# The low parts of split weights move from GpSimd to VectorE in each layer's first block

## The chip, the cores and the metric

The kernel runs on one core of one Trainium2 chip. The metric is device time in microseconds (us) of one execution of the whole program. Engines carry the names of the profile: PE (TensorE matmul), PEld (its weight loads), DVE (VectorE), ACT (ScalarE), POOL (GpSimd), SP (SyncE, which here only issues DMAs).

## What is computed

Two layers over one sequence of 2048 frames of width 1024. Each layer modulates and normalises its input, projects it once with a wide weight, runs two branches (gated linear attention and differential softmax attention) and projects their outputs back.

```python
for l in range(DEPTH):                       # DEPTH = 2
    mod = silu(c) @ w_ada[l] + b_ada[l]
    shift, scale, gate = jnp.split(mod, 3, axis=-1)
    h = rms_norm(x, norm_g[l]) * (1.0 + scale[:, None]) + shift[:, None]
    proj = h @ w_in[l]
    gq, gk, gv, glr, gz, dq, dk, dv, dz = split_columns(proj)
    gqkv = silu(causal_depthwise_conv(concat(gq, gk, gv), conv_w[l]))   # 4 taps
    o_gla = gla_branch(gqkv, glr, gz, ...)
    o_diff = diff_branch(dq, dk, dv, dz, ...)
    y = concat(o_gla, o_diff) @ w_out[l]
    x = x + gate[:, None] * y
```

## The kernel before

**Tiling.** The sequence is cut into four blocks of 512 frames (`u` = 0 to 3), so the program passes eight blocks, four for each layer (`l`). A block's dense work is nine items of eight weight tiles (`k`), each tile 128 x 512: four attention heads, two convolution groups and one gate from `w_in`, and two halves of `w_out`.

**Split weights.** Matmuls run on float32r, so each operand is kept as a high part (a rounded copy, float32r) and a low part (what is left of the float32 value), and three matmuls take the place of one: high by high, high by low, low by high. For a weight tile `weights()` does that (lines 586 to 599). In a layer's first block (`u` = 0) the raw tile comes in by DMA (`raw`, three buffers, 256 KB), ACT makes the high part into the first half of `w`, POOL subtracts it from `raw` to make the low part in the second half (line 596), and SP writes both halves to DRAM (`wd`, 512 KB). In the three later blocks the ready pair is read back (`w<-wd`) and no engine computes on it. `w` has four buffers. So the subtraction is done 2 layers x 9 items x 8 tiles = 144 times.

**Other work on these engines.** DVE does the convolution taps and their activation (`conv_evac`, tiles `ub`, `t`, `uT`, `qT`), the scores' maximum and copy out of PSUM (`s<-sc`), the mixing of the two softmax maps (`s<-s,r`), the low parts of the activations (`hlo`, `ql`, `ol`) and small statistics (`oss`, `qss`, `r`). POOL does small powers (`rq`, `wq`, `gw`, `xrs`), 64 x 64 memsets of `s`, and two kinds of 128 x 512 operation on tiles, `vN` and `rt`. `am` sums the columns of `w_ada` on DVE. `oh` and `ol` are the high and low part of the output projection's other operand, two buffers each.

**Order.** Operations are first recorded; `Program.order()` (line 199) then simulates the engines with a table of costs (`Program.cost`, line 171) and gives each engine the order in which it would take them, lowest recorded number first among those ready. Every engine then runs its list strictly in that order and waits at the first entry that isn't ready. For a 128 x 512 subtraction the planner reckons 100 + 2.2 x 512 = 1226 ns on POOL and 1.042 x 512 + 68 = 601 ns on DVE. SP's list is one queue as well: a `wd` write waits there for the low part, and the `raw` and `w<-wd` reads recorded after it wait behind it. All recorded operations carry line 305 (`issue`) in the profile, so they are told apart by their tiles.

Of the kernel before, what the change touches and what calls it, by code (L numbers as in the profile page):

```python
# [11 lines left out]
F32 = mybir.dt.float32  # L12
# [3 lines left out]
ALU = mybir.AluOpType  # L16
# [292 lines left out]
def trunk_kernel(ctx, tc, x, c, w_ada, b_ada, norm_g, w_in, conv_w, w_gk, b_gk, gla_norm_g,  # L309
# [28 lines left out]
    V, A, G, T, SY = (prog.queue(e) for e in "VAGTS")  # L338
# [247 lines left out]
    def weights(l, u, item, k, src, n=None):  # L586
        w = p_w.tile([P, 2, 512], F32R, tag="w", name="w")
        hi, lo = w[:, 0, :], w[:, 1, :]
        kept = WD[l][item][k]
        if u > 0:  # L590
            SY.dma_start(w.bitcast(F32), kept)
            return hi, lo
        raw = p_raw.tile([P, 512], F32, tag="raw", name="raw")
        SY.dma_start(raw if n is None else raw.rearrange("p (g n) -> p g n", n=n), src)
        A.copy(hi, raw)
        G.tensor_tensor(lo, raw, hi.bitcast(F32), op=ALU.subtract)
        if NU > 1:
            SY.dma_start(kept, w.bitcast(F32))
        return hi, lo
# [69 lines left out]
    def proj_T(l, u, item, col, banks):  # L669
        hhi, hlo = state["hhi"], state["hlo"]  # L670
        for k in range(KT):
            hi, lo = weights(l, u, item, k, w_in[l, k * P:(k + 1) * P, col:col + 512])
            for j in range(4):
                cs = slice(j * P, (j + 1) * P)
                if k == 0:
                    banks.append(acc())
                T.matmul(banks[j], hi[:, cs], hhi[k], start=(k == 0), stop=False)
                T.matmul(banks[j], hi[:, cs], hlo[k], start=False, stop=False)
                T.matmul(banks[j], lo[:, cs], hhi[k], start=False, stop=(k == KT - 1))
                yield pe(0.65)  # L680
# [387 lines left out]
    def dense_gen(l, u, items):  # L1068
# [12 lines left out]
        def head_proj(hd):  # L1081
            def ld(k):
                src = w_in[l, k * P:(k + 1) * P, C_D:C_D + 2048].rearrange("p (g n) -> p g n", n=512)
                return weights(l, u, hd, k, src[:, :, hd * P:hd * P + P], n=P)

            banks = []
            yield from proj_N(ld, banks)
            if hd == LAST:
                done("free_h", key + 1)
            if hd >= 1:  # L1090
                yield need("qkT", key, hd - 1)
            if hd >= 2:
                yield need("attn", key, hd - 2)
            head_evac(l, u, hd, banks)
            done("hev", key, hd)

        def gate_proj():
            banks = []
            yield from proj_N(lambda k: weights(l, u, 6, k, w_in[l, k * P:(k + 1) * P, C_GZ:C_GZ + 512]), banks)
            if LAST == 4:  # L1100
                done("free_h", key + 1)
            yield need("scan", key)
            osb = GL["osb"]
            for t in range(TT):
                sz = t2()
                silu2(sz, banks[t])
                G.tensor_tensor(osb[:, t, :], osb[:, t, :], sz, op=ALU.mult)
            done("gz", key)
# [135 lines left out]
```

## Time and profile before

| what | value |
|---|---|
| median of 3 runs | 2620.98 us (2617.81 to 2625.61) |
| the profiled execution's own time | 2622.21 us |
| its span in the profile | 2620.5 us |
| granted TensorE clock, mean | 0.992 |
| high parts `w` on ACT | 144, median 620 ns |
| low parts `w` on POOL | 144, median 1294 ns, longest 2534 ns |
| first and last low part start | 23.7 and 1620.3 us |

The profile is of one execution. A row of busy times counts an engine as busy from an instruction's start to its end, whether it computes or is held up in the middle. The rows of a group give its count, its total and the mean of one; the rows of waits give how long an engine stood idle and what ended it; the chain of waits follows the end of the program back to what released each step. The two stretches in which low parts are made are called the first and the second stage here: 20 to 340 us and 1310 to 1640 us.

### The profile page before, as it was taken

Reading aid. Unit: us, or ns where it says so; the run is one execution under the profiler, and the core shown is the slowest. Engines: PE = TensorE matmul, PEld = TensorE weight load, DVE = VectorE, ACT = ScalarE, POOL = GpSimd, SP = SyncE. Lnnn points to the kernel's source line nnn. Section 1 sums busy time; section 2 is a strip of 40 time slices with the busy share of each in tenths; the row PEclk is TensorE's granted clock in tenths of the full one; section 3 lists DMA queues with packets and bytes.
Section 4 is the critical chain, followed back from the end, with each engine's and each line's share of the span. In section 5 each row is a group of like instructions: output and inputs, shape, how many; then the busy total and the mean of one; then the engine's idle time right before and its main releaser. Section 6 shows DMA issues by size and latency. Waiting matters only on the chain.

```text
span 2620.5 us, 40701 instructions
## 1 busy us (share of the span) xinstructions
PE 2495.5 (95%) x13923; PEld 2031.5 (78%) x13923; DVE 1771.3 (68%) x5021; ACT 1215.3 (46%) x2592; POOL 608.3 (23%) x804
## 2 busy tenths in 40 slices
PE   6899899999999999999899999999999999999997
PEld 4676678877888778888677777888788887888786
DVE  4778847874667846677847874657737787377854
ACT  3555623554345543545634564344624556244442
POOL 2445421122010210102144554111111112110111
PEclk9999999999999999999999999999999999999998
DMA  8677586446553455344267767454374443743342
GB/s 283 225 235 256 200 302 198 161 166 211 178 181 125 158 171 189 133 140 149 81 237 248 245 214 253 169 179 156 126 268 155 143 157 113 254 141 129 101 149 89
DMA packets 201615, 476.11 MB, mean 182 GB/s; under 512 B 20736, under 2 KB 78272, under 8 KB 201408
## 3 DMA queue, kind: packets, MB, share of 16 engines
q1 hardware_dynamic: 201408, 473.51, 53.6%
q8 instruction: 111, 1.82, 0.3%
q14 instruction: 96, 0.79, 0.1%
HBM read 362.29 MB, written 111.15 MB: 181 GB/s over the span
## 4 chain that ended last, share of the span: by engine, by line
PE 71%; DVE 17%; DMA 3%; ACT 3%; issue 3%; POOL 1%; SPq 1%; DVEq 0%; ACTq 0%; POOLq 0%
PE acc L305 46%; PE sc L305 10%; PE po L305 8%; PE tp L305 7%; DVE s L305 6%; DVE t L305 3%; DMA wr<-in_w_ada_dram 1%; ACT s L305 1%; SPq L305 1%; DVE ql L305 1%; DVE am L305 1%; DVE hhi L305 1%; DMA w<-wd 1%; DVE r L305 1%; DVE hlo L305 1%
## 5 line engine op out<-in xcount | busy, mean ns | idle before, releaser
L305 PE MATMUL acc<-w,hhi 128*128 128x512 f32 x2560 | 835.0, 402 | 8.7 <-DMA w<-wd 4.3
L305 PEld LDWEIGHTS acc<-w,hhi 128*128 128x128 f32 x2560 | 464.8, 189 | 101.1 <-ACT ub L305 6.8
L305 PE MATMUL acc<-w,hlo 128*128 128x512 f32 x1280 | 504.9, 395 | 0.0
L305 ACT ACTIVATE s<-s,mx 128x512 f32<-128x512 f32 (+15 forms) x256 | 308.1, 1204 | 375.1 <-DVE s L305 372.3
L305 PE MATMUL acc<-hhi,w 128*128 128x512 f32 x1024 | 370.3, 402 | 0.6 <-DVE z L305 0.3
L305 PE MATMUL acc<-w,oh 128*128 128x512 f32 x1024 | 331.9, 401 | 12.1 <-DVE t L305 6.0
L305 DVE TENSOR_SCALAR_CACHE_REDUCE s<-sc,mx 64x64 f32<-64x64 f32 (+5 forms) x640 | 307.1, 485 | 37.8 <-PE sc L305 19.3
L305 POOL MEMSET s<- 64x64 f32 x256 | 38.9, 156 | 1111.1 <-DVE s L305 575.6
L305 PEld LDWEIGHTS acc<-w,hlo 128*128 128x128 f32 x1280 | 241.5, 189 | 48.9
L305 POOL TENSOR_TENSOR w<-raw,w 128x512 fp32r<-128x512 f32 x144 | 195.0, 1363 | 197.1 <-ACT w L305 180.7
L305 PEld LDWEIGHTS acc<-w,oh 128*128 128x128 f32 x1024 | 190.6, 190 | 55.8 <-DVE t L305 11.0
L305 PEld LDWEIGHTS acc<-hhi,w 128*128 128x128 f32 x1024 | 192.4, 188 | 37.7 <-DVE z L305 1.4
L305 PE MATMUL po<-Vj,aT 128*128 128x128 f32 x1536 | 207.9, 280 | 13.1 <-ACT aT L305 12.2
L305 PEld LDWEIGHTS po<-Vj,aT 128*128 128x128 f32 x1536 | 193.7, 195 | 24.6 <-ACT aT L305 18.9
L305 ACT COPY aT<-tp 128x512 f32<-128x512 f32 (+2 forms) x320 | 162.4, 520 | 94.1 <-PE tp L305 90.6
L305 PE MATMUL acc<-w,ol 128*128 128x512 f32 x512 | 202.8, 401 | 1.2 <-DVE ol L305 1.1
L305 DVE TENSOR_SCALAR_CACHE_REDUCE s<-sc 128x512 f32<-128x512 f32 (+4 forms) x256 | 158.6, 623 | 65.7 <-PE sc L305 61.6
L305 DVE SCALAR_TENSOR_TENSOR s<-s,r 128x512 f32<-128x512 f32 (+2 forms) x320 | 200.7, 677 | 3.1
L305 PE MATMUL acc<-hlo,w 128*128 128x512 f32 x512 | 200.9, 392 | 0.0
L305 PE MATMUL tp<-ident,s 128*128 128x128 f32 x1088 | 171.8, 275 | 16.9 <-DVE s L305 11.6
L305 POOL TENSOR_TENSOR rq<-qss,mhalf 128x4 f32<-128x4 f32 x128 | 129.8, 1032 | 215.4 <-DVE qss L305 215.3
L305 PEld LDWEIGHTS tp<-ident,s 128*128 128x128 f32 x1088 | 130.5, 140 | 55.4 <-issue 12.3
(177 smaller groups left out, 4064.7 us busy)
## 6 DMA issues: line engine op xcount, KB each, us to landing
w<-wd SPq DMA_DIRECT2D x432, 512.0 KB
wd<-w SPq DMA_DIRECT2D x144, 512.0 KB
raw<-in_w_in_dram SPq DMA_DIRECT2D x112, 256.0 KB
Kj<-kd SPq DMA_DIRECT2D x48, 512.0 KB
wr<-in_w_ada_dram SPq DMA_DIRECT2D x128, 128.0 KB
kd<-Kt SPq DMA_DIRECT2D x24, 512.0 KB
Vj<-vd SPq DMA_DIRECT2D x48, 256.0 KB
xt<-in_x_dram SPq DMA_DIRECT2D x16, 512.0 KB
```

Source lines behind the costliest of these rows:

```text
L305: getattr(self.engines[e], method)(*[real(a) for a in args], **{k: real(v) for k, v in kw.items()})
```

## The change

The subtraction that makes a weight's low part is issued on VectorE. The operands, the buffers and the rest of POOL's work stay.

```diff
         A.copy(hi, raw)
-        G.tensor_tensor(lo, raw, hi.bitcast(F32), op=ALU.subtract)
+        V.tensor_tensor(lo, raw, hi.bitcast(F32), op=ALU.subtract)
         if NU > 1:
             SY.dma_start(kept, w.bitcast(F32))
```

The planner sets a new order from it. Outside the two stages the orders of the engines hardly differ; within them the 144 subtractions stand among DVE's operations.

The first place is DVE's list at the end of the second convolution group of the first layer (`t` are the running taps, `uT` the activated result, `z`, `ol` belong to other streams). Before:

```order
L305 SCALAR_TENSOR_TENSOR t_1872<-ub,vec,t_1872 128x512
L305 TENSOR_SCALAR t_1916<-ub,vec 128x512
L305 COPY ub<-halo_142 128x3
L305 SCALAR_TENSOR_TENSOR t_1916<-ub,vec,t_1916 128x512
L305 SCALAR_TENSOR_TENSOR uT<-t_1920,t_1872 128x512
L305 SCALAR_TENSOR_TENSOR t_1916<-ub,vec,t_1916 128x512 x2
L305 TENSOR_TENSOR ol<-oT,oh 128x512
```

The same place in DVE's list now:

```order
L305 SCALAR_TENSOR_TENSOR t_1881<-ub,vec,t_1881 128x512
L305 TENSOR_SCALAR t_1924<-ub,vec 128x512
L305 TENSOR_TENSOR w<-raw,w 128x512
L305 SCALAR_TENSOR_TENSOR t_1924<-ub,vec,t_1924 128x512
L305 SCALAR_TENSOR_TENSOR uT<-t_1930,t_1881 128x512
L305 SCALAR_TENSOR_TENSOR t_1924<-ub,vec,t_1924 128x512
L305 TENSOR_TENSOR w<-raw,w 128x512
L305 SCALAR_TENSOR_TENSOR t_1924<-ub,vec,t_1924 128x512
L305 TENSOR_TENSOR w<-raw,w 128x512
L305 TENSOR_TENSOR ol<-oT,oh 128x512
```

Three subtractions (`w<-raw,w`) stand between the last taps of the group. In the four convolution groups of the two stages there are 5, 4, 2 and 4 of them between the first tap and the last activation.

The second place is DVE's list in the scores of the first attention head, first layer (`sc` is the scores' PSUM tile, `r` the softmax ratio). Before:

```order
L305 TENSOR_TENSOR Kt<-tp,Kt 64x512 x2
L305 TENSOR_SCALAR s,mx<-sc 128x64
L305 TENSOR_SCALAR s,mx<-sc,mx 64x64
L305 TENSOR_SCALAR s,mx<-sc 128x64
L305 SCALAR_TENSOR_TENSOR r<-ls 128x1
L305 TENSOR_SCALAR s,mx<-sc,mx 64x64
L305 TENSOR_SCALAR s,mx<-sc 128x192
L305 RECIPROCAL r<-ls 128x1
```

Now:

```order
L305 TENSOR_TENSOR Kt<-tp,Kt 64x512 x2
L305 TENSOR_TENSOR w<-raw,w 128x512
L305 TENSOR_SCALAR s,mx<-sc 128x64 x2
L305 TENSOR_SCALAR s,mx<-sc,mx 64x64 x2
L305 TENSOR_TENSOR w<-raw,w 128x512
L305 SCALAR_TENSOR_TENSOR r<-ls 128x1
L305 TENSOR_SCALAR s,mx<-sc 128x192
L305 RECIPROCAL r<-ls 128x1
L305 TENSOR_TENSOR w<-raw,w 128x512
```

Each `w<-raw,w` waits there for ACT's high part of the same tile, and the score operations that stand behind it wait with it.

The third place is the end of the second stage, where the output projection of the second layer's first block takes its last weights (`t<-acc,gate` are the outputs of the half before). On POOL the list before was as follows; `rt` adds the residual:

```order
L305 TENSOR_TENSOR rt<-t_16819,rt 128x512
L305 TENSOR_TENSOR rt<-t_16828,rt 128x512
L305 TENSOR_TENSOR rt<-t_16842,rt 128x512
L305 TENSOR_TENSOR rt<-t_16851,rt 128x512
L305 TENSOR_TENSOR w<-raw,w 128x512 x7
```

On DVE the list is now:

```order
L305 TENSOR_TENSOR t_16857<-acc,gate_14011 128x512
L305 TENSOR_TENSOR w<-raw,w 128x512
L305 TENSOR_TENSOR ol<-oT,oh 128x512
L305 TENSOR_TENSOR w<-raw,w 128x512 x2
L305 TENSOR_TENSOR ol<-oT,oh 128x512 x2
L305 TENSOR_TENSOR w<-raw,w 128x512
L305 TENSOR_TENSOR ol<-oT,oh 128x512
L305 TENSOR_TENSOR w<-raw,w 128x512
```

The subtractions no longer stand behind the four `rt`; they alternate with `ol`, which waits for ACT's `oh`.

## The prediction

> **What bounds the kernel now.** I read the page's totals first, then the chain that ended last, then the two stages in which the subtractions run.
>
> ```profile
> PE 2495.5 (95%) x13923; PEld 2031.5 (78%) x13923; DVE 1771.3 (68%) x5021; ACT 1215.3 (46%) x2592; POOL 608.3 (23%) x804
> PE 71%; DVE 17%; DMA 3%; ACT 3%; issue 3%; POOL 1%; SPq 1%; DVEq 0%; ACTq 0%; POOLq 0%
> ```
>
> PE is busy for 95% of the span and carries 71% of the chain; DVE carries 17%, POOL 1%. The subtractions sit in two stretches only. The next view gives the busy time of all engines in each (PE, PEld, DVE, ACT, POOL), and then, in its last two rows, that of the instructions that touch `raw` (ACT, POOL).
>
> ```profile
> 20.00:340.00 320.00, 285.56 (x1525) 214.94 (x1523) 235.17 (x611) 166.58 (x386) 145.98 (x155) 0.98 0.72 241
> 1310.00:1640.00 330.00, 307.96 (x1577) 243.65 (x1578) 210.21 (x534) 157.55 (x373) 160.66 (x166) 0.99 0.70 239
> 20.00:340.00 320.00, 44.23 (x72) 97.83 (x72) 0.98 0.72 241
> 1310.00:1640.00 330.00, 44.48 (x72) 97.13 (x72) 0.99 0.70 239
> ```
>
> PE idles 320 - 285.56 = 34.4 us in the first stage and 330 - 307.96 = 22.0 us in the second, 56.5 us together: by making PE idle less, the change can win no more than that. DVE is busy 445.4 of 650 us (69%). The clock is 0.98 and 0.99 there, so it is not what moves. In the later blocks nothing of the change runs, and I expect nothing of it there.
>
> **What DVE's time consists of.** This is the timeline of the second convolution group of the first layer, first POOL, then DVE (start, duration).
>
> ```profile
> 176.12 4.34 POOL L305 TENSOR_TENSOR w<-raw,w 128x512 fp32r<-128x512 f32 x3 [1.35 <-ACT w L305]
> ...
> 164.51 0.48 DVE L305 TENSOR_SCALAR t<-ub,vec 128x512 f32<-128x512 f32 x1
> 171.50 0.16 DVE L305 COPY ub<-halo 128x3 f32<-128x3 f32 x1
> 171.62 0.75 DVE L305 SCALAR_TENSOR_TENSOR t<-ub,vec,t 128x512 f32<-128x512 f32 x1
> 176.53 1.52 DVE L305 TENSOR_SCALAR t<-ub,vec 128x512 f32<-128x512 f32 x1
> 177.97 1.26 DVE L305 COPY ub<-halo 128x3 f32<-128x3 f32 x1
> 179.15 1.86 DVE L305 SCALAR_TENSOR_TENSOR t<-ub,vec,t 128x512 f32<-128x512 f32 x1
> 182.97 0.69 DVE L305 TENSOR_TENSOR ol<-oT,oh 128x512 fp32r<-128x512 f32 x1
> 183.57 0.16 DVE L305 COPY ub<-halo 128x3 f32<-128x3 f32 x1
> ```
>
> The three operations that take 0.48, 0.16 and 0.75 us by themselves take 1.52, 1.26 and 1.86 us while POOL makes three low parts: 3.25 us more for three, about 1.1 us each. So a subtraction on POOL that meets DVE work costs DVE more than DVE would need for it: `ol<-oT,oh`, the same subtraction at the same size, has 0.69 us, and the next instruction starts 0.60 us behind it.
>
> **Term 1, what is added to DVE.** 144 x 0.60 us = 86 us (99 us by the full 0.69 us, which overlaps its neighbour).
>
> **Term 2, what is taken from DVE.** Not every low part meets DVE work. For each form of DVE operation I took its mean in the stage less its mean in the quiet stretch 420 to 1290 us, times its count. Two of the largest are these, the stage first, then the quiet stretch:
>
> ```profile
> L305 DVE SCALAR_TENSOR_TENSOR am<-wr,cact,am 128x256 f32<-128x256 f32 x42 | 27.2, 647 | 5.0 <-DMA wr<-in_w_ada_dram 4.7
> L305 DVE TENSOR_TENSOR rw<-rw,rq 128x256 f32<-128x256 f32 x16 | 12.6, 790 | 3.1 <-POOL rq L305 3.1
> ...
> L305 DVE SCALAR_TENSOR_TENSOR am<-wr,cact,am 128x256 f32<-128x256 f32 x29 | 14.0, 482 | 7.6 <-DMA wr<-in_w_ada_dram 7.2
> L305 DVE TENSOR_TENSOR rw<-rw,rq 128x256 f32<-128x256 f32 x44 | 18.4, 420 | 6.4 <-POOL rq L305 6.2
> ```
>
> `am` gives 42 x 0.165 = 6.9 us, `rw` 16 x 0.370 = 5.9 us; all forms give 37.5 us in the first stage and 29.1 in the second, 66.6 us. So DVE's load rises by 86 - 66.6, about 20 us net in 650, to some 72%. What matters is where.
>
> **The convolution groups.** In the four groups of the two stages DVE is the bound (columns as above):
>
> ```profile
> 97.00:124.00 27.00, 22.33 (x112) 17.34 (x111) 25.69 (x59) 14.23 (x35) 14.35 (x18) 1.00 0.67 210
> 157.00:184.00 27.00, 24.24 (x125) 19.08 (x123) 25.66 (x59) 15.14 (x35) 11.96 (x15) 1.00 0.53 169
> 1390.00:1418.00 28.00, 24.01 (x119) 18.71 (x118) 26.23 (x64) 13.62 (x34) 13.52 (x17) 1.00 0.55 175
> 1457.00:1478.00 21.00, 18.63 (x99) 14.70 (x98) 20.70 (x45) 11.65 (x26) 10.86 (x13) 1.00 0.59 190
> ```
>
> DVE is busy 98.3 of 103 us, and PE idles 103 - 89.2 = 13.8 us. Read as above, 24 DVE operations there are lengthened, by 21.7 us in all (the first is below: an `oss` of 0.15 us takes 0.91). The new order has 5, 4, 2 and 4 subtractions there, 15 x 0.60 = 9.0 us. DVE's work falls by 12.7 us. PE cannot gain all of it, since it idles 13.8 us and part of that has other causes; I take two thirds, **-8.5 us** (bounds 0 and -12.7).
>
> ```profile
> 97.75 0.91 DVE L305 SCALAR_TENSOR_TENSOR oss<-oss,r 128x1 f32<-128x1 f32 x1
> ```
>
> **Low parts on the chain.** These are pieces of the chain in order of time, then one POOL row of the timeline and the stretch's busy times.
>
> ```profile
> 267.54 1.79 POOL w L305
> 1539.03 1.29 POOL w L305
> 1601.18 1.32 POOL rt L305
> 1602.50 2.92 POOL w L305 x2
> 1610.12 1.31 POOL w L305
> 1620.33 1.29 POOL w L305
> ...
> 1596.92 5.58 POOL L305 TENSOR_TENSOR rt<-t,rt 128x512 f32<-128x512 f32 x4 [3.52 <-DVE t L305]
> 1596.87 1.13 ACT L305 CAST w<-raw 128x512 fp32r<-128x512 f32 x2
> 1600.00:1640.00 40.00, 36.16 (x156) 28.56 (x155) 7.47 (x11) 6.12 (x10) 16.88 (x13) 1.00 0.87 302
> ```
>
> The first two go from 1.79 and 1.29 to 0.69 us each, 1.7 us. At 1600 us two low parts whose high parts were ready at 1598.0 wait until 1602.5 for four `rt` on POOL; SP's writes and the next raw reads wait behind them. On DVE, idle most of that time (7.47 of 40 us), they start some 3 to 4 us earlier and run half as long. PE idles only 40 - 36.16 = 3.8 us there, which caps it. I take 1.2 + 3.5 = **-4.7 us** (bounds 0 and -5.5).
>
> **Everywhere else.** There remain 129 x 0.60 = 77.4 us added and 66.6 - 21.7 = 44.9 us taken off: +32.5 us on a DVE that is busy 347 of 547 us outside the groups. Most of it falls into DVE's gaps while PE has dense matmuls; if the cover is gone, all of it counts. DVE carries 17% of the whole chain; I charge one part in eight, as these operations are mostly made ahead of their use: **+4 us** (bounds 0 and +32.5).
>
> Powers on POOL no longer queue behind low parts; DVE's `rw` waits 3.1 us for `rq` in the whole first stage (row above), so I count nothing. SP's list keeps its kinds of transfers, and the low part is the last thing that a `wd` write waits for, as before.
>
> Sum: -8.5 - 4.7 + 4 = **-9.2 us**. Against the profiled execution's 2622.2 us that gives 2613.0; the median stands 1.2 us below that execution, so I forecast **2612 us** for the median.
>
> A page speaks against the change: the Trainium skill, "Perfetto Trace Analysis", section "Optimizing Scalar/DVE Operations", says that where DVE is saturated, moving work off it, even to GpSimd, may make sense; by that alone the 9.0 us put into the saturated groups would be a loss, and the sum 9.0 - 4.7 + 4 = +8 us; the third rival below is its case. The same section warns that the two engines share a port, and the Trainium skill, "SBUF — State Buffer", section "SBUF: two separate sides", calls that an exclusive lock held for a whole instruction; the lengthened rows at 176 us agree, and by it the groups gain.
>
> **Rivals.**
>
> *Given back (no change).* The groups' gain is not passed on, because the dense matmuls wait for ACT or for PSUM instead, and the charge elsewhere is higher: half of -8.5, -3 of -4.7, +6 elsewhere, about -1 us: 2620. For it speaks that PE is already 90% busy in the groups (89.2 of 103 us); against, that they end with PE waiting for `uT`.
>
> *Head of the line (slower).* On POOL a low part that waits for its high part holds up little. On DVE the scores and the softmax ratio stand behind it, then ACT's exponentials and PE's transposes. The rows of waits price it:
>
> ```profile
> POOL w L305 <- ACT w L305: 180.7, 70, 11.6
> ACT w L305 <- PE acc L305: 37.0, 24, 3.8
> ACT w L305 <- DMA raw<-in_w_in_dram: 25.9, 16, 5.7
> ACT w L305 <- DMA raw<-in_w_out_dram: 4.2, 5, 1.9
> ```
>
> POOL stood idle 180.7 us for high parts, mostly with nothing behind; ACT itself was held 37.0 + 25.9 + 4.2 = 67 us by a full `w` buffer or a late raw tile. DVE inherits these holds where it gets there first. If it takes half, 33 us, and half of that reaches PE, it costs 17 us: -9.2 + 17 = +8, so 2629. It decides from about 18 us of DVE idle on PE's account. Against it: when ACT is held by PE, PE is busy, and DVE is late more often than early at 72% load.
>
> *The lengthening has another cause.* If DVE's long operations were not due to POOL's low parts, DVE would carry 86 us more with no relief: +9.0 in the groups, -4.7, and an eighth of 77 elsewhere, +14 us: 2635. POOL's powers speak against it: one runs 1.01 us from 197.68, and a DVE operation with two SBUF operands in the middle of it takes its usual 0.42.
>
> ```profile
> 197.68 1.01 POOL L305 TENSOR_TENSOR rq<-qss,mhalf 128x4 f32<-128x4 f32 x1 [0.48 <-DVE qss L305]
> 198.03 0.42 DVE L305 TENSOR_TENSOR rw<-rw,rq 128x256 f32<-128x256 f32 x1
> ```
>
> So it is large POOL operations that lengthen, and the low parts are 144 of them.
>
> **How the numbers follow.** Forecast 0.46, given back 0.33, head of the line 0.17, another cause 0.04. A measurement of this kernel can tell about 0.3% (7.9 us) from no change. Faster by over 0.3% takes the forecast: 0.46; within it, the given-back case: 0.33; slower, the two others: 0.21. The forecast's own range takes the favourable bounds, -12.7 - 5.5 + 0 = -18 us (2603), and to be open to a further gain elsewhere as large as the net +4 us charged I go to 2599; upward the range reaches into the head-of-line case, to 2630.
>
> **What would show it.** DVE's `w<-raw,w` at 0.69 us, x144; `t<-ub,vec,t`, `am` and `rw` back at 0.75, 0.48 and 0.42 us in the stages; the groups shorter by 2 to 3 us each; PE's idle time at 1600 to 1640 us nearly gone; DVE busy about 465 us in the two stages. I am wrong if waits of DVE's `w` for ACT's `w` pass 18 us and PE's idle time rises above 56.5 us, or if the four groups do not shorten.

## The result and the profile after

| | before | after |
|---|---|---|
| median | 2619.39 us (2617.61 to 2625.61, 4 runs) | 2598.18 us (2594.80 to 2600.39, 4 runs) |
| ratio, 95% interval | | 0.9914 [0.9893, 0.9934] |
| the profiled execution's own time, its span | 2622.21, 2620.5 us | 2597.78, 2595.6 us |

The kernel is 21 us faster, well past the 0.3% that can be told from no change. 2612 was forecast: the sign was right, the gain is more than twice the forecast, and the time lies just below the range's 2599.

The page's totals of the changed kernel, and the shares of the chain that ended last:

```profile
PE 2491.2 (96%) x13923; PEld 2036.9 (78%) x13923; DVE 1792.7 (69%) x5165; ACT 1213.2 (47%) x2592; POOL 422.0 (16%) x660
PE 76%; DVE 14%; ACT 3%; DMA 3%; issue 2%; SPq 1%; POOL 1%; DVEq 0%; ACTq 0%; POOLq 0%
```

DVE has 144 instructions more and only 21 us more of busy time, and the chain runs through it less (14% where it was 17%). Busy times in the two stages (PE, PEld, DVE, ACT, POOL, as in the prediction):

```profile
20.00:340.00 320.00, 297.75 (x1585) 228.62 (x1585) 244.43 (x691) 164.86 (x386) 56.58 (x86) 0.98 0.76 260
1310.00:1640.00 330.00, 317.07 (x1610) 253.68 (x1608) 227.85 (x616) 158.76 (x380) 70.06 (x94) 0.99 0.74 255
```

PE idles 320 - 297.75 = 22.3 us and 330 - 317.07 = 12.9 us, **35.2 us together, 21.3 less than before**. Outside the two stages PE idles as long as it did (125.0 - 56.5 = 68.5 us before, 104.4 - 35.2 = 69.2 us now, by span less PE's busy time), so the gain lies in the stages, as the prediction had it. The two profiled executions differ by 24.9 us in span, more than the medians' 21; what the idle time leaves over is PE's busy time, 4.3 us lower. Next the stretches that hold the four convolution groups, of the same lengths as the prediction's; the second layer's work now comes some 15 us earlier, so its two are shifted.

```profile
97.00:124.00 27.00, 26.86 (x138) 22.26 (x137) 25.56 (x68) 15.64 (x36) 3.65 (x9) 1.00 0.73 232
157.00:184.00 27.00, 27.00 (x165) 22.00 (x164) 23.30 (x60) 14.94 (x32) 2.32 (x5) 1.00 0.67 222
1374.00:1402.00 28.00, 23.54 (x119) 19.16 (x119) 26.09 (x74) 14.53 (x36) 4.09 (x11) 0.95 0.48 155
1445.00:1466.00 21.00, 20.89 (x111) 17.10 (x110) 18.82 (x43) 13.59 (x29) 2.47 (x4) 1.00 0.54 172
```

PE is busy 98.3 of 103 us and idles 4.7, where it idled 13.8. From first tap to last activation the four groups take 72.8 us, where they took 81.7. The timeline of the second group shows why (DVE rows: start, duration):

```profile
163.32 0.48 DVE L305 TENSOR_SCALAR t<-ub,vec 128x512 f32<-128x512 f32 x1
163.71 0.16 DVE L305 COPY ub<-halo 128x3 f32<-128x3 f32 x1
163.83 0.75 DVE L305 SCALAR_TENSOR_TENSOR t<-ub,vec,t 128x512 f32<-128x512 f32 x1
...
169.92 0.69 DVE L305 TENSOR_TENSOR w<-raw,w 128x512 fp32r<-128x512 f32 x1
170.52 0.76 DVE L305 SCALAR_TENSOR_TENSOR t<-ub,vec,t 128x512 f32<-128x512 f32 x1
```

The same three kinds of operation that took 1.52, 1.26 and 1.86 us beside low parts on POOL take 0.48, 0.16 and 0.75, and a subtraction holds the next tap for 0.60 us. The end of the second stage:

```profile
1575.00:1615.00 40.00, 38.83 (x170) 31.18 (x169) 17.42 (x26) 10.01 (x17) 11.08 (x8) 1.00 0.83 297
```

PE idles 1.2 of 40 us there, where it idled 3.8. The instructions that touch `raw` answer the head-of-line rival: the duration of a low part (shortest, median, longest), and further down the idle time of the engines before these instructions, with the time that ended by a high part, and how often.

```profile
L305 DVE TENSOR_TENSOR w<-raw,w x144: 668/686/1793, 23.6 to 1595.1; 128x512 fp32r<-128x512 f32 x144
...
  ACT w L305: 27.3, 22
```

The idle time of PE that went is thus 13.8 - 4.7 = 9.1 us in the groups, 3.8 - 1.2 = 2.6 us at the end, and the rest, 21.3 - 11.7 = **9.6 us, everywhere else**, where the prediction had a loss of 4.

### The profile page after: what moved, and what is told of

Same layout as the page of the kernel before. It is cut to its first block, busy times and chain, and to the rows that moved or that the text cites. A ratio compares the mean times of both kernels' runs of the same rounds, so it can differ in the third digit from the quotient of the medians.

```text
span 2595.6 us, 40663 instructions
## 1 busy us (share of the span) xinstructions
PE 2491.2 (96%) x13923; PEld 2036.9 (78%) x13923; DVE 1792.7 (69%) x5165; ACT 1213.2 (47%) x2592; POOL 422.0 (16%) x660
## 4 chain that ended last, share of the span: by engine, by line
PE 76%; DVE 14%; ACT 3%; DMA 3%; issue 2%; SPq 1%; POOL 1%; DVEq 0%; ACTq 0%; POOLq 0%
PE acc L305 49%; PE sc L305 11%; PE po L305 9%; PE tp L305 7%; DVE s L305 5%; DVE t L305 2%; DMA wr<-in_w_ada_dram 1%; SPq L305 1%; DVE ql L305 1%; DVE w L305 1%; ACT s L305 1%; DVE hhi L305 1%; DMA Kj<-kd 1%; DVE Kt L305 1%; DMA raw<-in_w_in_dram 0%
## 5 line engine op out<-in xcount | busy, mean ns | idle before, releaser
L305 PE MATMUL po<-Vj,aT 128*128 128x128 f32 x1536 | 208.7, 281 | 13.0 <-ACT aT L305 12.1
L305 PE MATMUL sc<-Kj,qh 128*128 128x512 f32 x384 | 158.4, 412 | 7.6 <-DVE s L305 2.6
```

What stands on the lines that cost most here:

```text
L305: getattr(self.engines[e], method)(*[real(a) for a in args], **{k: real(v) for k, v in kw.items()})
```

## The experiments

Three explanations of that gain elsewhere stand against each other. A: DVE's operations are no longer lengthened there either, and that counted. B: the low part is ready sooner. C: the planner's new order. A fourth, D, came up with the first results: POOL's own queue is free. Each kernel ran in turns with the kernel before on the same chip, and the ratio is to that. Not all of them ran on one chip; the medians of the kernel before are 2618.7 to 2620.2 us in these sets:

| kernel | median, us | ratio to before, 95% interval |
|---|---|---|
| e1, order alone | 2623.8 | 1.0013 [1.0000, 1.0025] |
| e2, engine alone | 2607.1 | 0.9955 [0.9941, 0.9968] |
| e3, lengthening back | 2625.0 | 1.0024 [1.0013, 1.0034] |
| e4, low part late | 2617.8 | 0.9989 [0.9978, 1.0001] |
| e5, POOL occupied | 2602.9 | 0.9933 [0.9915, 0.9952] |
| e6, `vN` on DVE too | 2588.7 | 0.9882 [0.9863, 0.9901] |
| e7, `rt` on DVE too | 2598.9 | 0.9922 [0.9906, 0.9938] |
| e8, both | 2590.2 | 0.9885 [0.9867, 0.9903] |
| e9, items 1 and 2 only | 2609.1 | 0.9954 [0.9937, 0.9971] |
| e10, all but items 1 and 2 | 2606.4 | 0.9950 [0.9936, 0.9963] |
| e11, reckoned at 686 ns | 2597.5 | 0.9907 [0.9893, 0.9921] |
| e12, reckoned at 1226 ns | 2601.5 | 0.9926 [0.9910, 0.9941] |
| e13, added work doubled | 2644.3 | 1.0100 [1.0083, 1.0117] |

Where "lengthened" has a total below, each DVE operation's duration was compared with the quickest tenth of its form in the changed kernel, and what it took beyond that was put down to the POOL operation beside it. Before the change that gives 66.1 us in 78 operations beside low parts, 18.4 beside `vN` and 11.7 beside `rt`; after it 0, 18.9 and 12.9.

### Order and engine apart: e1 and e2

Both keep the list of one kernel and change only on which engine the subtraction is issued. e1, from the changed kernel (e2 does the reverse from the kernel before):

```diff
+            e = self.swap.get(i, e)
...
+        prog.swap[len(prog.ops)] = "G"
         V.tensor_tensor(lo, raw, hi.bitcast(F32), op=ALU.subtract)
```

> The changed kernel's order of every engine is kept word for word, but the 144 subtractions are issued on GpSimd again, at the places of VectorE's list merged into GpSimd's. If the planner's new order alone makes the gain (theory C): about 2598 to 2604 us, near the changed kernel. If the gain comes from VectorE no longer being lengthened (A) or from the low part being ready sooner (B): 2615 us or more, as before the change, with the vector operations lengthened again.

> The order that was planned for GpSimd is kept, but the 144 subtractions are issued on VectorE at the places that order gives them. Engine alone, no new plan. Theories A (VectorE no longer lengthened) and B (low part ready sooner): 2596 to 2604 us. Theory C (the new order): 2612 us or more. A head-of-line hold on VectorE, as the plan reckons 1226 ns where 690 are needed, would show as waits of VectorE for the high part above the 27 us of the changed kernel.

The order alone gains nothing: C falls as the whole cause. The engine alone gains 12 us by its ratio, 13 by its median. That lies between the bands that were given for A and B and for C. So 9 to 11 of the change's 21 to 22 us come only when the new order and the new engine meet. In e1 78.7 us of DVE time are lengthened by low parts, more than before, as that order sets them beside DVE's work.

### The low part later, and the lengthening back: e3 and e4

e3 and e4 add to the changed kernel, behind the subtraction:

```diff
+        for j in range(5):                                   # e3
+            part = hi.bitcast(F32)[:, 96 * j:96 * j + 96]
+            G.tensor_tensor(scr, part, part, op=ALU.subtract)
...
+        G.tensor_tensor(scr, lo[:, 0:4].bitcast(F32), two, op=ALU.pow)   # e4
+        G.tensor_tensor(lo[:, 0:4], raw[:, 0:4], hi[:, 0:4].bitcast(F32), op=ALU.subtract)
```

> The changed kernel, and beside each subtraction GpSimd makes five subtractions of 128x96 from the high part into a scratch tile that nobody reads (together about as long as one low part took there; the planner reckons them at nothing). The low part is ready as soon as in the changed kernel. Theory A: the vector operations are lengthened again, by some 60 us in all, and 10 us or more of the 21 are lost: 2608 to 2622 us. Theory B: no loss beyond 3 us: 2598 to 2602 us. If five short operations do not lengthen VectorE's as one long did, it tells nothing on A.

> The changed kernel, but behind each subtraction on VectorE GpSimd takes one power of 128x4 from the low part into a scratch tile, and then writes the first four columns of the low part once more. The low part counts as ready some 1.5 to 2 us later and again behind GpSimd's other work, and no large GpSimd operation lengthens VectorE's. Theory B: most of the gain is lost, 2608 to 2620 us. Theory A: it stays, 2598 to 2603 us.

e3 loses all of the gain and 5 us more, beyond A's band, and e4 loses nearly all; neither tells as much as was hoped. e3 lengthens DVE's operations by only 27.0 us (180 operations), but POOL's load also went to 439.8 us in the two stages (126.6 in the changed kernel):

```profile
20.00:340.00 320.00, 286.33 (x1512) 216.23 (x1505) 256.84 (x677) 165.62 (x386) 214.16 (x440) 0.97 0.71 238
1310.00:1640.00 330.00, 303.71 (x1570) 240.12 (x1569) 242.00 (x607) 160.01 (x375) 225.60 (x455) 0.99 0.68 236
```

The first stage's `rw`, with the idle time of DVE before it:

```profile
L305 DVE TENSOR_TENSOR rw<-rw,rq 128x256 f32<-128x256 f32 x16 | 7.4, 464 | 6.3 <-POOL rq L305 6.2
```

DVE waits 6.2 us for `rq`, which waits on POOL behind the scratch work (1.4 us in the changed kernel). Lengthening and POOL's queue are mixed; e5 was made for that. In e4 PE waits openly for the late low part, first stage, then second (total, times, longest):

```profile
PE acc L305 <- POOL w L305: 10.7, 11, 1.7
...
PE acc L305 <- POOL w L305: 8.0, 5, 4.6
```

So lateness can cost as much as the change gains, and e4's time lies in B's band. But lateness isn't what the change removed. From the starts and ends of the `w` rows, in order of time and without the first three of a stage, the mean from a high part's end to its low part's end is as follows (in e4 to the end of the four columns that are written once more; e5 and e13 come further down):

| | before | after | e1 | e2 | e4 | e5 | e13 |
|---|---|---|---|---|---|---|---|
| first stage, us | 2.1 | 3.1 | 3.2 | 1.8 | 4.7 | 3.1 | 5.5 |
| second stage, us | 2.2 | 2.5 | 2.4 | 1.8 | 4.7 | 2.5 | 4.5 |

In the changed kernel the low part is made in half the time and ready *later*, as it stands in DVE's queue. So B is not what the change gained: PE waited 0.9 and 2.1 us in the two stages for a low part before, and now waits 0.9 us in the first and in the second

```profile
PE acc L305 <- DVE w L305: 2.9, 1, 2.9
```

In e2, in the old order, the low part is ready 0.3 to 0.4 us sooner than before. PE's waits for it fall from 3.0 to 1.9 us there (0.4 in the first stage, 1.5 in the second), so B can account for about 1 of e2's 12 to 13 us.

### POOL occupied, nothing lengthened: e5

```diff
         V.tensor_tensor(lo, raw, hi.bitcast(F32), op=ALU.subtract)
+        G.tensor_tensor(scr, hi.bitcast(F32)[:, 0:6], mhalf[:, 0:6], op=ALU.pow)
```

> The changed kernel, and beside each subtraction GpSimd makes one power of 128x6 from the high part into a scratch tile that nobody reads (some 1.35 us, as long as a low part took there; the planner reckons it at nothing). GpSimd is as occupied as before the change, but no vector operation should be lengthened and the low part is not later. Theory D (what the change bought is GpSimd's free queue: rsqrt powers, masks and products no longer stand behind low parts): 10 us or more of the 21 are lost, 2608 to 2620 us. Theory A (the lengthening of vector operations was what cost): 2598 to 2603 us, and the 27 us that the five short subtractions lost beside the changed kernel are then lengthening rather than queue.

```profile
L305 POOL TENSOR_TENSOR scr<-w,mhalf x144: 1314/1336/3656, 23.6 to 1596.7; 128x6 f32<-128x6 f32 x144
```

POOL is as busy as before the change (342.8 us in the two stages, 306.6 before), not one DVE operation is lengthened by these powers, and 2602.9 us remain. So D is worth some 5 us by the medians, and as the intervals of e5 and of the changed kernel overlap, perhaps nothing. e5 and e1 have the same order on DVE, PE and ACT and of SP's transfers, row for row, if the subtractions and the scratch powers are left aside. POOL's load is no lower in e5 (342.8 us, 306.1 in e1), and the low parts are about equally late (table above). What is left is one difference: in e5 DVE does the 144 subtractions, in e1 it is lengthened by them. e5 is 20.9 us faster. That is A. (How e3's loss of 27 us divides stays open: its POOL load is larger still.)

### Where the gain is: e9 and e10

The low parts that are made in and around the groups are those of weight items 1 and 2 of each layer.

```diff
-        V.tensor_tensor(lo, raw, hi.bitcast(F32), op=ALU.subtract)
+        (V if item in (1, 2) else G).tensor_tensor(lo, raw, hi.bitcast(F32), op=ALU.subtract)   # e9
```

> Only the 32 low parts of the weight items that are made around the four convolution groups (items 1 and 2 of both layers) go on VectorE; the other 112 stay on GpSimd. By the prediction's own terms: the groups' 8.5 us, so 2609 to 2613 us. By theory A: the groups' 7.5 us that the traces show and no more, 2609 to 2615 us. It tells the theories apart together with the next kernel.

> The other way round: the 112 low parts away from the groups go on VectorE, the 32 of items 1 and 2 stay on GpSimd. By the prediction's own terms (4.7 us gained on the chain, 4 us lost elsewhere) nothing is left: 2617 to 2622 us. Theory A (the lengthening elsewhere is on the path as well, the added work lies in gaps): 10 to 16 us gained, 2602 to 2610 us.

e9 gains 12.1 us [7.6, 16.5], e10 13.1 us [9.7, 16.8] (ratios times 2620.2); together 25. The whole change gains 22.5 us by its own ratio, the same within these intervals. In e10 the four groups stay as they were before (busy times around them, columns as above):

```profile
106.00:127.00 21.00, 15.48 (x75) 12.04 (x74) 20.92 (x41) 10.34 (x24) 9.19 (x9) 0.95 0.61 209
167.00:187.00 20.00, 17.51 (x91) 13.72 (x90) 19.47 (x38) 11.02 (x25) 8.23 (x8) 1.00 0.50 162
1395.50:1416.50 21.00, 17.66 (x80) 14.24 (x81) 20.57 (x41) 8.25 (x16) 8.30 (x9) 0.92 0.47 151
1454.50:1473.50 19.00, 17.66 (x94) 14.08 (x93) 18.88 (x35) 10.92 (x25) 7.67 (x8) 1.00 0.55 179
```

DVE is busy 79.8 of 81 us, and PE, busy 68.3, idles 12.7. So e10's 13 us come from outside the groups alone: the place where the prediction had -4.7 + 4 = about nothing.

### What an added microsecond costs: e13

```diff
         V.tensor_tensor(lo, raw, hi.bitcast(F32), op=ALU.subtract)
+        for j in range(4):
+            part = hi.bitcast(F32)[:, 96 * j:96 * j + 96]
+            V.tensor_tensor(scr, part, part, op=ALU.subtract)
```

> The changed kernel, and behind each subtraction VectorE makes four subtractions of 128x96 from the high part into a scratch tile that nobody reads: about 0.6 us, so VectorE's added work is doubled once more by some 86 us, with the low part no later and nothing lengthened (planned at the table's cost). It gives the price of an added microsecond by itself. By the prediction's charge (one part in eight): 11 us slower than the changed kernel, 2609 us. Theory A with the rough weights of the other moves (an added microsecond counts about half): some 40 us, 2630 to 2645 us; with a third, 2620 to 2630 us.

```profile
PE 2505.9 (95%) x13923; PEld 2040.0 (77%) x13923; DVE 1902.3 (72%) x5741; ACT 1215.3 (46%) x2592; POOL 421.8 (16%) x660
```

DVE is busy 1902.3 - 1792.7 = 109.6 us more, and the kernel is 46 us slower: **0.42 us for each added one**. Theory A's band held, the charge of one in eight did not. But the low part did come later, against what was expected: 5.5 and 4.5 us behind the high part, as late as in e4 or later. How much of the 46 us is due to that was not separated. The load is also higher than the change's own, so for the change 0.42 is rather an upper end. With it, e1 and e5 price the lengthened microsecond: e5 carries 144 x 0.60 = 86 us added, 36 us at 0.42, and is still 20.9 us faster than e1 with its 78.7 us lengthened: (20.9 + 36) / 78.7 = **0.72**. Test on e2: 86 x 0.42 - 66.1 x 0.72 = -11.5 us; 12 to 13 were measured as a gain. The test is weak, since a lower price of the added microsecond lowers the other with it: at nothing for the added one, the lengthened one is 20.9 / 78.7 = 0.27 and e2 would gain 17.6. So the two prices are estimates, bound to one another by e1 and e5.

### The order's part: e11 and e12

Only the planner's cost of the subtraction on DVE changes (601 ns in the change):

```diff
+        prog.ops[-1] = prog.ops[-1][:5] + (686.0,) + prog.ops[-1][6:]     # e11; 1226.0 in e12
```

> The changed kernel, with the planner told 686 ns for a low part on VectorE (its measured time) where its table has 601 ns. If the part of the gain that comes with the new order (some 9 us between the order made for GpSimd and the changed kernel) follows from knowing the engine, it stays: 2594 to 2602 us. If it is the luck of one order, any other will do as well or worse: 2600 to 2610 us.

> The changed kernel, with the planner told 1226 ns for a low part on VectorE, as it reckoned on GpSimd. The low parts are placed in VectorE's list with the engine known and the duration wrong. If the order's part of the gain comes from knowing that VectorE does them, 2596 to 2604 us; if from knowing that they are short, 2604 to 2612 us, near the engine alone in the old order (2607).

e11 has another order in the stages and the same time, so the order's part isn't the luck of one list. e12 loses some 3 us, within the intervals. Most of the order's part, then, seems to need only that the planner knows on which engine the subtraction runs. In e12 the four groups take 81.7 us from first tap to last activation, as long as before the change, but PE idles only 5.1 us in them (12.5 before, 4.7 in the changed kernel): so the length of a group alone doesn't tell what PE loses in it.

The planner also set a new order for e9 and e10. With the lengthening that is left in them (47.1 and 24.2 us beside low parts), the two prices alone give gains of 6 and 2 us, where 12.1 and 13.1 were measured. So in these two kernels, as well, a large part of the gain seems to come with the order. Which places of the order bring it was not separated further; one is seen: from the 4224th to the 4416th of PE's matmuls into `acc`, the end of the second stage, the changed kernel gains 3.3 us on the kernel before, and e2 only 0.6.

### The rest of the lengthening: e6, e7 and e8

```diff
-                G.tensor_tensor(osb[:, t, :], osb[:, t, :], sz, op=ALU.mult)
+                V.tensor_tensor(osb[:, t, :], osb[:, t, :], sz, op=ALU.mult)     # e6, e8
...
-                G.tensor_tensor(rt[:, t, :], gy, rt[:, t, :], op=ALU.add)
+                V.tensor_tensor(rt[:, t, :], gy, rt[:, t, :], op=ALU.add)        # e7, e8
```

> The changed kernel, with the gate product vN (32 of 128x512, line 1107) on VectorE too. Its runs on GpSimd still lengthen vector operations by 18.9 us in all, 24 times; on VectorE it adds 32 x 0.60 = 19 us. Theory A with the weights the first runs suggest (a lengthened microsecond counts nearly in full, an added one little): 2585 to 2594 us. If added and lengthened microseconds count alike: 2596 to 2600 us.

> The changed kernel, with the residual sum rt (60 of 128x512, line 1152) on VectorE too. On GpSimd it lengthens vector operations by 12.9 us, 20 times; on VectorE it adds 60 x 0.60 = 36 us. Theory A as above: 2588 to 2597 us. If both count alike: 2599 to 2610 us.

> Both of the two moves at once: no 128x512 operation is left on GpSimd, no vector operation is lengthened, and VectorE carries 55 us more. Theory A: 2575 to 2592 us, the sum of the two alone. If both count alike: 2600 to 2612 us.

**e6 beats both kernels: 2588.7 us, 9.5 less than the change.** This is the timeline of the changed kernel where `vN` runs on POOL (`hhi` and `hlo` are the high and low part of the activation tile that PE's next matmuls read):

```profile
1226.41 2.60 POOL L305 TENSOR_TENSOR vN<-vN,t 128x512 f32<-128x512 f32 x2 [1.77 <-DVE t L305]
1227.04 2.11 DVE L305 CAST hhi<-t 128x256 fp32r<-128x256 f32 x2
...
1230.50 2.59 POOL L305 TENSOR_TENSOR vN<-vN,t 128x512 f32<-128x512 f32 x2 [1.50 <-DVE oss L305]
1231.11 0.84 DVE L305 CAST hhi<-t 128x256 fp32r<-128x256 f32 x1
1231.99 1.39 DVE L305 TENSOR_TENSOR hlo<-t,hhi 128x256 fp32r<-128x256 f32 x1
```

and of e6 at the same place:

```profile
1219.49 0.49 DVE L305 CAST hhi<-t 128x256 fp32r<-128x256 f32 x2
1219.90 0.76 DVE L305 TENSOR_TENSOR hlo<-t,hhi 128x256 fp32r<-128x256 f32 x2
1220.57 1.29 DVE L305 TENSOR_TENSOR vN<-vN,t 128x512 f32<-128x512 f32 x2
```

Two casts take 2.11 us beside `vN` and 0.49 without. e6 adds 32 x 0.60 = 19 us to DVE and takes 15 off it (18.9 less 3.9 that `rt` lengthens more): by the two prices that is 8 - 11 = -3 us, and -9.5 came by the medians (-8.4 by the ratios). It may be that what sits right ahead of PE, as these casts do, counts above 0.72; but the planner set a new order here as well, and the two were not separated. e7 adds 36 us and takes 13 off: 15 - 9 = +6 by the prices, +0.8 measured. A's 2588 to 2597 for e7 was missed, and e8, both moves at once, has the time of e6. `rt` can stay where it is.

## Why the prediction was right and wrong

**The convolution groups, -8.5: right.** `t<-ub,vec,t` is back at 0.75 us, PE's idle time there fell by 9.1 us, and the groups are 2.2, 2.1, 3.2 and 1.4 us shorter, where 2 to 3 each were foretold. That PE can't gain all of DVE's 12.7 us held.

**Low parts on the chain, -4.7: about right** where it can be read: the end of the second stage gave 2.6 us of PE's idle time (3.3 in progress) for 3.5. But e2 gives 0.6 there, so it came by the order, not by the engine's speed alone.

**Terms 1 and 2: right.** `w<-raw,w` has 686 ns, 144 times. In the first stage of the changed kernel:

```profile
L305 DVE SCALAR_TENSOR_TENSOR am<-wr,cact,am 128x256 f32<-128x256 f32 x46 | 23.3, 506 | 10.3 <-DMA wr<-in_w_ada_dram 9.9
...
L305 DVE TENSOR_TENSOR rw<-rw,rq 128x256 f32<-128x256 f32 x16 | 6.8, 422 | 1.5 <-POOL rq L305 1.4
```

`am` came back to 506 ns, `rw` to 422. DVE's busy time in the stages rose to 472.3 us, against 465 foretold; more work falls into the same stretches now.

**Everywhere else, +4 (bounds 0 and +32.5): this step failed.** It was a gain, 9.6 us by PE's idle time and 13.1 us in e10, which holds the chain's term too. Two things were wrong in it. First, added and lengthened microseconds were netted at one price, and one part in eight was charged on what was left. The runs price them apart, at about 0.42 us for an added one and 0.72 for a lengthened one; that an added subtraction can more often wait, while something already waits for a lengthened operation, is a reading of these two prices and was not seen by itself. By them 77.4 x 0.42 - 44.9 x 0.72 is about 0. That is rather too high, as 0.42 is an upper end: in e2 PE idles 8.1 us less in the groups than before (4.4 against 12.5 us, from first tap to last activation), which leaves 4 to 5 of its 12 to 13 us for all else. So the bound at 0, below which the step saw nothing, had no reason. Second, the new order was given no worth outside the places that were named. It brings 9 to 11 us, 3 of them at the end of the second stage. How the 9.6 us divide exactly between the two stays open.

**The rivals.** *Head of the line* did not come: DVE waits 27.3 us for high parts, above the 18 from which it was to decide, but PE's idle time fell to 35.2 us. The threshold was wrong in that it counted DVE's waits as PE's. *Given back* and *another cause* are excluded by the groups and by the lengthened rows that are gone.

**What spoke against the change.** The Trainium skill, "Perfetto Trace Analysis", section "Optimizing Scalar/DVE Operations", lets work be moved off a saturated DVE, even to GpSimd, and warns of the shared port. Here the warning decided: in the very groups in which DVE is full, PE's idle time fell by 9.1 us when subtractions were put on it. The Trainium skill, "SBUF — State Buffer", section "SBUF: two separate sides", has the operation that starts first hold that port to its end; the rows at 1231 us agree (1.39 us for an `hlo` whose usual time, in e6, is 0.42, and which ends 0.29 us after `vN` does); e5's powers, of 1.34 us each, lengthened nothing and don't agree.

## What to carry to other kernels

Work on GpSimd isn't free because GpSimd is idle: count what its large operations add to VectorE's, and where those stand. Price added work and lengthened work apart, and don't net them before pricing. Where a planner sets the order, time the engine change with and without the new order, since nearly half of the gain lay in their meeting here.

## What the runs showed of the hardware

- GpSimd's busy time alone doesn't lengthen; it depends on the operation. The 128 x 512 subtractions of 1.29 us lengthened 78 of DVE's operations by 66.1 / 78 = 0.85 us each; the short ones of e3 (128 x 96, 348 ns at the median) lengthened 180 by 27.0 / 180 = 0.15 us each, and the 144 powers of 128 x 6, 1336 ns each, lengthened none. Whether the power's kind or its few elements spare DVE, no run tells.
- Tiny operations are held as well: `oss<-oss,r` on 128 x 1 took up to 1.26 us beside `vN`, against 0.15.
- Casts with one operand in SBUF are held too: `hhi<-t` took up to 1.39 us, against 0.28.
- Not every operation is held. Before the change `t<-acc,gate`, which reads PSUM, ran 45 times beside a 128 x 512 operation on GpSimd, and `s<-sc`, which does too, 24 times; none took more than 0.02 us beyond its usual time.
